# One word per load instead of one per row, and the weights issued behind the barrier: a router kernel

## The chip, the core and the metric

The kernel runs on one core of a Trainium2 chip. The core has five engines with an instruction stream each: TensorE (PE in the profile; PEld is its weight load), VectorE (DVE), ScalarE (ACT), GpSimd (POOL) and SyncE (SP). They meet at semaphores only. DMAs are issued by SyncE, ScalarE or GpSimd and run on sixteen DMA engines. The metric is the device time in microseconds (us), the median of several runs.

## The reference

```python
batch, seq, dim = 16, 512, 1024;  num_loras = 8          # x, router_weights: float32
logits = np.matmul(x, router_weights)                     # 8192 x 1024 times 1024 x 8
exp_logits = np.exp(logits - np.max(logits, axis=-1, keepdims=True))
return (exp_logits / np.sum(exp_logits, axis=-1, keepdims=True)).astype(np.float32)
```

A tall matrix product with eight columns, and a softmax over each row of eight. The input is 32 MB and the output 0.26 MB.

## The kernel before

The 8192 rows are laid out as 128 partitions by 64; "row j" means the j-th row of every partition, so a row is a tile of 128 x 1024 elements. Rows 0 to 3 come as float32 into `x_f32` (two DMAs of SyncE) and ScalarE casts them. All other rows are cast to bfloat16 by the DMA itself, issued by GpSimd: twelve loads of four rows, three of two, five of one (`LOADS`), and row 63 in three pieces of four, two and two eighths (`PIECES`). Each load has its own semaphore, `s_ld[i]` or `s_z[i]`. GpSimd issues all of them in the first 17 us, without waiting for anything but the barrier.

Work on a row: TensorE transposes its eight 128 x 128 chunks (a "turn", against `identity`), into PSUM. VectorE copies five of them to SBUF (`xTv`, L378) and ScalarE three (`xTs`, L351). Then TensorE multiplies the eight transposed chunks with the weights (`multiply`, L238) into eight columns of `lg`. After each group of eight rows VectorE and ScalarE make the softmax between their copies. The last four rows are done one by one (`alone`), the last of them in pieces (L310, L324), and SyncE stores the output in two DMAs (L160, L162).

The order on every engine is written by hand. TensorE's main part is a loop of 31 trips of two rows, with addresses in registers. A trip is: `loop_turn(1)` for an odd row, `multiply` of the even row before it, `loop_turn(0)` for the next even row, a branch, two filler matmuls, and `multiply` of the odd row. The buffers alternate by the parity of the row.

Three things are touched here:

- **Words.** TensorE is told by SyncE that a row of x is there. For each row from 2 to 62 SyncE waits for the load (or the cast) if the row begins one, and adds one to a semaphore (L157): for an even row to `s_in`, for which TensorE waits ahead of `loop_turn(0)` (L295); for an odd row to `s_c[1]`, which also counts the two copies of the odd row before it. So the multiply of an odd row waits for three: its own two copies, and the word of the next odd row (`want=3`). So that this count isn't run ahead of, SyncE waits for `s_tv`, TensorE's count of turned rows, ahead of each odd row.
- **The first turn.** It waits for two casts (`s_cast`, L275).
- **The weights.** ScalarE issues their load (L137) beside SyncE's two loads of x_f32, before `tc.close()` (L144), which makes all engines meet at a barrier. TensorE turns the weights as soon as they and `ident` are there (L268 to L270), and VectorE casts them to `w_bf`.

Of the kernel before, what the change touches and what calls it, by code (L numbers as in the profile page):

```python
# [11 lines left out]
def kernel(  # L12
# [6 lines left out]
    nc = tc.nc  # L19
# [5 lines left out]
    KO = D // P  # L25
    J = M // P
# [13 lines left out]
    LOADS = [4] * 13 + [2, 2, 2] + [1] * 5  # L40
# [14 lines left out]
    def sb(name, shape, dtype):  # L55
        size = mybir.dt.size(dtype)
        for n in shape[1:]:
            size *= n
        at = place[0]
        place[0] = -(-(at + size) // 64) * 64  # L60
        return nc.alloc_sbuf_tensor_at(name, shape, dtype, offset=at).ap()
# [9 lines left out]
    w8 = sb("w8", [KO, P, N], fp32)  # L71
# [24 lines left out]
    sem = tc.alloc_semaphore  # L96


    s_f = [nc.alloc_semaphore(f"s_f{i}") for i in range(2)]
    s_w = nc.alloc_semaphore("s_w")  # L100
    s_ld = [sem(f"s_ld{i}") for i in range(len(LOADS))]
    s_z = [sem(f"s_z{i}") for i in range(len(PIECES))]
    s_cast = sem("s_cast")
# [7 lines left out]
    s_tv = sem("s_tv")  # L111
    s_ts = sem("s_ts")
    s_c = [sem(f"s_c{i}") for i in range(2)]
    s_in = sem("s_in")
# [10 lines left out]
    first = [sum(LOADS[:i]) for i in range(len(LOADS))]  # L125
# [3 lines left out]
    with tc.manual_schedule():  # L129
        early = [  # L130
            nc.sync.dma_start(
                out=x_f32[:, 2 * i:2 * i + 2, :], in_=x_rows[:, 2 * i:2 * i + 2, :]
            ).then_inc(s_f[i], 16)
            for i in range(2)
        ]
        early.append(
            nc.scalar.dma_start(  # L137
                out=w8, in_=router_weights.rearrange("(ko ki) n -> ko ki n", ko=KO)
            ).then_inc(s_w, 16)
        )  # L140
        for t in early:
            tc.no_tile_sem_insts.add(t.ins.name)
    tc.close()
# [2 lines left out]

    sp = nc.sync


    for j in range(2, J - 1):  # L150
        if j % 2:
            sp.wait_ge(s_tv, j - 1)
        if j < LOADS[0]:
            sp.wait_ge(s_cast, j + 1)
        elif j in first:
            sp.wait_ge(s_ld[first.index(j)], 16)
        sp.sem_inc(s_c[1] if j % 2 else s_in, 1)  # L157
    sp.wait_ge(s_z[0], 16)
    sp.wait_ge(s_out, NG - 1)
    sp.dma_start(out=out_rows[:, 0:DONE, :], in_=outv[:, 0:DONE, :]).then_inc(s_st[0], 16)  # L160
# [6 lines left out]
    for i, r in enumerate(LOADS):  # L167
        if i:
            nc.gpsimd.dma_start(  # L169
                out=xa[:, first[i]:first[i] + r, :], in_=x_rows[:, first[i]:first[i] + r, :]  # L170
            ).then_inc(s_ld[i], 16)
        if i == 2:
# [3 lines left out]
                out=ident, in_=ident, compare_op=ALU.not_equal, fill=1.0, base=0,  # L176
# [10 lines left out]
    pe = nc.tensor  # L187
# [7 lines left out]
    def at(ap, like, r):  # L195
        return mybir.RegisterAccessPattern(
            ap=ap, dtype=like.dtype, memsetref=like.tensor.name + "_set",
            regref=r.name, is_regloc_offset=False, reg_ap_offset=r.name,
            const_ap_offset=0, const_sub_tensor_id=0,
        )  # L200

    def again(like, **k):
        return pe.add_instruction(copy.replace(like, name=f"I-{nc.next_id()}", **k))

    def turn_ap(b, c):
        return (ptv if c < VN else pts)[b][:, c if c < VN else c - VN, :]

    def chunk(b, c):
        return xTv[b][:, c, :] if c < VN else xTs[b][:, c - VN, :]

    def loop_turn(b):

        for c in range(KO):
            t = again(
                turn_like,
                ins=(turn_like.ins[0], at([[J * D, P], [1, P]], xa, r_x[c])),
                outs=(pe.lower_ap(turn_ap(b, c), opt=False),),
            )
            if c == VN - 1:
                t.then_inc(s_tv, 1)  # L220
            if c == KO - 1:
                t.then_inc(s_ts, 1)
        pe.reg_add(r_l, r_l, 256)
        for c in range(KO):
            if c == KO // 2:
                pe.reg_alu(r_l, r_l, -4097, ALU.bitwise_and)
            pe.reg_add(r_x[c], r_x[c], D * 2)
# [7 lines left out]
                t.then_inc(s_ts, 1)  # L235
        return t

    def multiply(b, dst, want=2):  # L238

        for c in range(KO):  # L240
            if c == 0:
                pe.wait_ge(s_c[b], want).then_inc(s_c[b], -want)
            if dst is None:
                m = again(
                    mult_like,
                    ins=(
                        pe.lower_ap(w_bf[:, c, :], opt=False),
                        pe.lower_ap(chunk(b, c), opt=False, for_matmul_weights=True),
                    ),
                    outs=(at([[2 * G * 64, P], [1, N]], lg, r_l),),  # L250
                    start_tensor_calc=(c == 0),
                    stop_tensor_calc=(c == KO - 1),
                )
            else:
                m = pe.matmul(  # L255
                    dst, lhsT=chunk(b, c), rhs=w_bf[:, c, :],
                    start=(c == 0), stop=(c == KO - 1),
                )
            if c == KO - 1:
                m.then_inc(s_p, 1)  # L260

    def fill():
        return pe.matmul(spare, lhsT=filler[:, 0:P], rhs=filler, start=True, stop=True)  # L263
# [1 line left out]

    w_ps = lg[:, 1, 0:N, 0:KO]
    pe.wait_ge(s_id, 1)
    pe.wait_ge(s_w, 16).then_inc(s_w, -16)  # L268
    for n in range(N):
        t = pe.transpose(w_ps[:, n, :], w8[:, :, n], ident[0:KO, 0:KO])  # L270
    t.then_inc(s_wt, 1)
    pe.wait_ge(s_fill, 1)
    mult_like = fill().ins
    pe.wait_ge(s_idb, 1)
    pe.wait_ge(s_cast, 2)  # L275
    turn_like = pe.transpose(turn_ap(0, 0), xa[:, 0, 0:P], identity).ins  # L276
    turn(0)
    pe.wait_ge(s_wb, 1)
# [2 lines left out]
    def left_of(i):  # L281

        return X_AT + D * 2 * (2 * i + 3) + (P - 1) * 2
# [3 lines left out]
    with nc.body("rows_multiply", valid_engines=only_pe):  # L287
        fill()
        fill()
        multiply(1, None, want=3)  # L290
        pe.br("rows_turn")
    with nc.body("rows_turn", valid_engines=only_pe):
        loop_turn(1)
        multiply(0, None)
        pe.wait_ge(s_in, 1).then_inc(s_in, -1)  # L295
        loop_turn(0)
        pe.br_lt(r_x[0], left_of(TRIPS - 1), on_true="rows_multiply", on_false="rows_done")
    nc.switch_bb("rows_done")
# [14 lines left out]
    pe.wait_ge(s_c[(J - 3) % 2], 2)  # L313
    turn_piece(0)
    multiply((J - 3) % 2, alone[1])
    turn_piece(1)
    turn_piece(2)
# [13 lines left out]
    act = nc.scalar  # L331

    def cast(i):
        act.wait_ge(s_f[i], 16).then_inc(s_f[i], -16)  # L334
        for k in (2 * i, 2 * i + 1):
            act.copy(xa[:, k, :], x_f32[:, k, :]).then_inc(s_cast, 1)  # L336
# [12 lines left out]
    def act_copy(j):  # L349
        act.wait_ge(s_ts, j + 1)  # L350
        act.copy(xTs[j % 2], pts[j % 2][:, 0:SN, :]).then_inc(s_c[j % 2], 1)  # L351

    cast(0)
    for j in range(J - 3):
        act_copy(j)
# [67 lines left out]
    for j in range(J - 3):  # L423
# [26 lines left out]
        out=outv[:, J - ALONE:J, :], in0=ev3, in1=inv3.broadcast_to([P, ALONE, N]), op=ALU.mult  # L450
# [31 lines left out]
```

## Time and profile before

| | |
|---|---|
| runs before | 86.65, 86.79, 86.89, 86.90 us; median 86.84 |
| profiled execution | 86.75 us, of which its span is 85.4 |
| busy | PE 64.1 us (75%), PEld 52.7 (62%), DVE 38.9 (46%), ACT 38.1 (45%), POOL 13.5 (16%) |
| HBM read, written | 33.59 MB, 0.26 MB |
| x_f loads | two of 1024 KB, issued from 0.74, 4.8 and 8.0 us to landing |
| three pieces of row 63 | issued from 15.0 to 16.1, 65.6 to 65.9 us to landing |
| mean granted TensorE clock | 0.977 of full speed |

The profile is one execution; its times are microseconds from its first instruction. Busy time is by engine. A group or wait names the line, the engine, the operation and the tiles (output before the arrow, input after it). In a waits view, "A <- B: total, times, longest" says that A waited for B. In a timeline the columns are the start, the duration, the engine (a q behind it means its instruction queue), the line, the operation, the tiles and, in brackets, the idle time before it with what ended that. The strip of 40 slices gives the busy share in tenths (9 is 90% or more). The queue lines give packets, MB, and the time of the packets as a share of sixteen engines' span. The trace also holds each DMA packet's start and duration by queue, and the times at which DMAs add to their semaphores; a load has landed when the last of them has come.

### The profile page before, as it was taken

To read this page: it belongs to the slowest core of one execution; us is meant where nothing else is said; L and a number is where in the kernel's file an instruction comes from. 1 tells how busy PE (TensorE), PEld (TensorE's weight loads), DVE (VectorE), ACT (ScalarE), POOL (GpSimd) and SP (SyncE) were. 2 spreads that over 40 slices of the span, in tenths; PEclk is the share of its full clock that TensorE was granted. 3 is DMA by queue.
4 is the path that set the end of the run, shared out by engine and by line. 5 is a ranking of instruction groups with operands and counts; after the bars stand their busy time and mean duration, and the time that the engine had idled before them with its cause. 6 is when DMAs were issued, how large, how long until landed. Compare 5 with 4: busy or idle time off the path is not lost. (4 is left out here: it accounts for less than half of the span.)

```text
span 85.4 us, 2849 instructions
## 1 busy us (share of the span) xinstructions
PE 64.1 (75%) x1094; PEld 52.7 (62%) x1094; DVE 38.9 (46%) x114; ACT 38.1 (45%) x81; POOL 13.5 (16%) x30
## 2 busy tenths in 40 slices
PE   0052739999995977949389997959598699999860
PEld 0040727888874755838258785847476488777650
DVE  0020222466574542745226554636347257665662
ACT  0039385454663352535223454524426246545470
POOL 0489999800000000000000000000000000000000
PEclk9999999999999999999975999999999999999998
DMA  2999999999999999999999999999999999999920
GB/s 58 338 430 307 230 188 238 192 238 199 234 196 234 196 234 196 238 196 234 199 230 203 226 207 222 215 215 219 211 219 198 213 215 215 198 211 208 172 101 23
DMA packets 3906, 18.14 MB, mean 212 GB/s; under 512 B 568, under 2 KB 1080, under 8 KB 2112
## 3 DMA queue, kind: packets, MB, share of 16 engines
q0 software_dynamic: 3312, 15.73, 90.1%
q1 hardware_dynamic: 576, 2.36, 7.2%
q10 hardware_dynamic: 16, 0.03, 0.2%
q14 instruction: 2, 0.02, 0.0%
HBM read 33.59 MB, written 0.26 MB: 396 GB/s over the span
## 5 line engine op out<-in xcount | busy, mean ns | idle before, releaser
L351 ACT COPY xTs<-pts 128x384 bf16<-128x384 bf16 x63 | 30.1, 479 | 38.1 <-PE pts L276 36.8
L378 DVE COPY xTv<-ptv 128x640 bf16<-128x640 bf16 x63 | 31.0, 492 | 34.0 <-PE ptv L276 29.8
L276 PE MATMUL ptv<-identity,x_all 128*128 128x128 bf16 x311 | 29.1, 226 | 12.5 <-SPq L157 8.5
L276 PEld LDWEIGHTS ptv<-identity,x_all 128*128 (+1 forms) x311 | 19.1, 100 | 13.7 <-issue 13.5
L276 PE MATMUL pts<-identity,x_all 128*128 128x128 bf16 x186 | 21.7, 228 | 0.0
L263 PEld LDWEIGHTS lg<-w_bf,xTv 128*128 128x128 bf16 x305 | 15.7, 99 | 8.1 <-issue 2.1
L263 PE MATMUL spare<-filler 128*128 128x512 bf16 x61 | 19.8, 407 | 0.6
L263 PE MATMUL lg<-w_bf,xTv 128*128 128x8 bf16 x305 | 16.7, 167 | 0.0
L276 PEld LDWEIGHTS pts<-identity,x_all 128*128 x186 | 13.9, 103 | 0.0
L263 PE MATMUL lg<-w_bf,xTs 128*128 128x8 bf16 x183 | 13.2, 166 | 0.0
L169 POOL DMA_DIRECT2D x_all<-in_x_dram x20 | 10.8, 602 | 2.8 <-POOLq L144 2.8
L263 PEld LDWEIGHTS lg<-w_bf,xTs 128*128 128x128 bf16 x183 | 9.0, 96 | 0.0
L263 PEld LDWEIGHTS spare<-filler 128*128 128x128 bf16 x61 | 4.6, 103 | 2.4 <-issue 2.3
L270 PE MATMUL lg<-ident,w 8*128 8x8 f32 x8 | 1.0, 251 | 5.3 <-PEq L268 5.3
L270 PEld LDWEIGHTS lg<-ident,w 8*128 8x128 f32 x8 | 0.9, 197 | 5.3 <-issue 5.3
L336 ACT CAST x_all<-x_f 128x1024 bf16<-128x1024 f32 x4 | 4.0, 1044 | 0.0
L336 ACT ACT_TABLE_LOAD x1 | 1.3, 1283 | 5.6 <-ACTq L334 5.6
L386 DVE TENSOR_REDUCE mx<-lg 128x8 f32<-128x64 f32 (+1 forms) x8 | 1.8, 221 | 4.3 <-PE lg L263 4.3
L372 DVE CAST identity<-ident 128x128 bf16<-128x128 f32 x1 | 0.5, 518 | 5.3 <-POOL ident L175 5.3
L341 ACT ACTIVATE ev<-ex 128x64 f32<-128x64 f32 (+1 forms) x8 | 2.0, 253 | 1.1 <-DVE ex L390 1.0
L182 POOL DMA_DIRECT2D x_all<-in_x_dram x3 | 1.7, 687 | 0.0
L390 DVE TENSOR_TENSOR ex<-lg,mx 128x64 f32<-128x64 f32 (+1 forms) x8 | 1.7, 212 | 0.0
(41 smaller groups left out, 15.9 us busy)
## 6 DMA issues: line engine op xcount, KB each, us to landing
x_all<-in_x_dram POOLq DMA_DIRECT2D x12, 1024.0 KB, 32.6
x_f<-in_x_dram SPq DMA_DIRECT2D x2, 1024.0 KB, 6.4
x_all<-in_x_dram POOLq DMA_DIRECT2D x3, 512.0 KB, 60.2
x_all<-in_x_dram POOLq DMA_DIRECT2D x5, 256.0 KB, 64.3
out_dram<-outv SPq DMA_DIRECT2D x1, 208.0 KB, 1.9
x_all<-in_x_dram POOLq DMA_DIRECT2D x1, 128.0 KB, 65.9
x_all<-in_x_dram POOLq DMA_DIRECT2D x2, 64.0 KB, 65.7
out_dram<-outv SPq DMA_DIRECT2D x1, 48.0 KB, 1.6
```

What stands on the lines that cost most here:

```text
L169: nc.gpsimd.dma_start(out=xa[:, first[i]:first[i] + r, :], in_=x_rows[:, first[i]:first[i] + r, :]).then_inc(s_ld[i], 16)
L182: nc.gpsimd.dma_start(out=xa[:, J - 1, c], in_=x_rows[:, J - 1, c]).then_inc(s_z[i], 16)
L263: return pe.matmul(spare, lhsT=filler[:, 0:P], rhs=filler, start=True, stop=True)
L270: t = pe.transpose(w_ps[:, n, :], w8[:, :, n], ident[0:KO, 0:KO])
L276: turn_like = pe.transpose(turn_ap(0, 0), xa[:, 0, 0:P], identity).ins
L336: act.copy(xa[:, k, :], x_f32[:, k, :]).then_inc(s_cast, 1)
L341: act.activation(ev[g % 2][:, 0:n, :], ex[g % 2][:, 0:n, :], func=Exp).then_inc(s_ev, 1)
L351: act.copy(xTs[j % 2], pts[j % 2][:, 0:SN, :]).then_inc(s_c[j % 2], 1)
L372: dve.tensor_copy(out=identity, in_=ident).then_inc(s_idb, 1)
L378: dve.tensor_copy(out=xTv[j % 2], in_=ptv[j % 2][:, 0:VN, :]).then_inc(s_c[j % 2], 1)
L386: dve.reduce_max(mx[b][:, 0:n, 0], rows, axis=X).then_inc(s_d, 1)
L390: dve.tensor_tensor(out=ex[b][:, 0:n, :], in0=rows, in1=mx[b][:, 0:n, :].broadcast_to([P, n, N]), op=ALU.subtract,).then_inc(s_ex, 1)
```

## The change

SyncE now adds to `s_in` alone: one for each of the four casts, and for every other load as many as it has rows, in one instruction when the load lands. It no longer looks at `s_tv`. TensorE takes one from `s_in` ahead of every turn, odd or even, so the wait goes into `loop_turn` itself; the multiply of an odd row waits for its two copies only. The first turn takes one from `s_in` too. The load of the weights goes from before the barrier to the head of ScalarE's own program behind it, ahead of the casts; its semaphore is one that the context clears, so TensorE no longer subtracts from it. The order of matmuls, copies and loads on each engine is the same in both kernels.

```diff
-    s_w = nc.alloc_semaphore("s_w")
+    s_w = sem("s_w")
...
-        early.append(
-            nc.scalar.dma_start(
-                out=w8, in_=router_weights.rearrange("(ko ki) n -> ko ki n", ko=KO)
-            ).then_inc(s_w, 16)
-        )
...
-    for j in range(2, J - 1):
-        if j % 2:
-            sp.wait_ge(s_tv, j - 1)
-        if j < LOADS[0]:
-            sp.wait_ge(s_cast, j + 1)
-        elif j in first:
-            sp.wait_ge(s_ld[first.index(j)], 16)
-        sp.sem_inc(s_c[1] if j % 2 else s_in, 1)
+    for j in range(LOADS[0]):
+        sp.wait_ge(s_cast, j + 1)
+        sp.sem_inc(s_in, 1)
+    for i, r in enumerate(LOADS):
+        if i:
+            sp.wait_ge(s_ld[i], 16)
+            sp.sem_inc(s_in, r)
...
     def loop_turn(b):
 
+        pe.wait_ge(s_in, 1).then_inc(s_in, -1)
         for c in range(KO):
...
-    def multiply(b, dst, want=2):
+    def multiply(b, dst):
...
-                pe.wait_ge(s_c[b], want).then_inc(s_c[b], -want)
+                pe.wait_ge(s_c[b], 2).then_inc(s_c[b], -2)
...
-    pe.wait_ge(s_w, 16).then_inc(s_w, -16)
+    pe.wait_ge(s_w, 16)
...
-    pe.wait_ge(s_cast, 2)
+    pe.wait_ge(s_in, 1).then_inc(s_in, -1)
...
-        multiply(1, None, want=3)
+        multiply(1, None)
...
         multiply(0, None)
-        pe.wait_ge(s_in, 1).then_inc(s_in, -1)
         loop_turn(0)
...
+    act.dma_start(
+        out=w8, in_=router_weights.rearrange("(ko ki) n -> ko ki n", ko=KO)
+    ).then_inc(s_w, 16)
     cast(0)
```

## The prediction

> **What bounds the kernel now.** I read the page first, for the share of the DMA queues and the strip of the 40 slices.
>
> ```profile
> span 85.4 us, 2849 instructions
> ...
> DMA  2999999999999999999999999999999999999920
> GB/s 58 338 430 307 230 188 238 192 238 199 234 196 234 196 234 196 238 196 234 199 230 203 226 207 222 215 215 219 211 219 198 213 215 215 198 211 208 172 101 23
> ...
> q0 software_dynamic: 3312, 15.73, 90.1%
> q1 hardware_dynamic: 576, 2.36, 7.2%
> q10 hardware_dynamic: 16, 0.03, 0.2%
> ```
>
> The sixteen DMA engines are full from the second slice to the 38th. Queue 1 carries rows 0 to 3 (x_f32) and the stores, queue 0 the other rows, queue 10 the weights: 0.2% of the engines' time. TensorE is busy 75%, VectorE and ScalarE 46% and 45%. So the load stream looks like the bound; the chain that ended last covers only 80.48 us onward and cannot say so. The waits do, TensorE's first, then SyncE's queue (total us, times, longest):
>
> ```profile
> PE ptv L276 <- SPq L157: 8.5, 8, 1.8
> ...
> SPq L157 <- DMA x_all<-in_x_dram: 36.6, 19, 3.7
> SPq L157 <- PE ptv L276: 27.7, 17, 2.4
> ```
>
> TensorE waits for SyncE's word, and SyncE for a load. Its second wait, 27.7 us for s_tv, only paces words of rows that are there already. The timeline shows that TensorE has caught up by 27.66:
>
> ```profile
> 0.74 0.58 ACTq L137 DMA_DIRECT2D w<-in_router_weights_dram  x1
> 0.74 0.86 SPq L131 DMA_DIRECT2D x_f<-in_x_dram  x2
> ...
> 5.32 1.01 PE L270 MATMUL lg<-ident,w 8*128 8x8 f32 x8 [5.32 <-PEq L268]
> ...
> 9.03 0.27 PE L276 MATMUL ptv<-identity,x_all 128*128 128x128 bf16 x1 [2.16 <-ACT x_all L336]
> ...
> 27.66 0.44 PE L276 MATMUL ptv<-identity,x_all 128*128 128x128 bf16 x5 [0.99 <-SPq L157]
> ...
> 80.52 0.44 PE L276 MATMUL ptv<-identity,x_all 128*128 128x128 bf16 x5 [0.30 <-PEq L295]
> ...
> 81.71 0.28 PE L310 MATMUL extra<-identity,x_all 128*128 128x128 bf16 x2
> ...
> 83.82 0.34 SPq L162 DMA_DIRECT2D out_dram<-outv  x1
> ```
>
> The same idle time follows with nearly every four-row load (1.06 before 32.52, 1.07 before 37.44, 1.81 before 43.06). At the end row 62 lands at 80.35 by the trace's semaphore records and is turned at 80.52. The last quarter row (s_z[2]) lands at 81.67 and is turned at 81.71. From that landing to the end of the span are 85.4 - 81.67 = 3.7 us that the diff does not touch. So end = end of the load stream + 3.7 us.
>
> **The change, part by part.** The sum is made on the profiled execution: 86.75 us, of which 85.4 are span and 1.35 lie around it. It is 0.09 below the median of the four runs, 86.84; the forecast is put on the median.
>
> *The words of SyncE.* 61 row words become 24 (four for the casts, twenty for loads). One costs 17 ns when it does not wait, on a queue that is not the bound. Row 62 still has a load and a word of its own (lands 80.35, SyncE's instruction at 80.37), so the last one is no sooner. Worth nothing.
>
> *The wait of an odd turn.* It leaves multiply's `want=3` and becomes an instruction in loop_turn(1): 31 more waits, at 51 ns each by the row of the same kind (L295), 1.6 us of TensorE's sequencer. Behind each queue that turn, the next multiply and the next even turn; VectorE and ScalarE wait for these. Per four-row load that is two, 0.10 us, under an idle time of 1.06 us. Every such load begins with an even row, whose wait stays where it is. Only rows 59 and 61 begin a load with an odd row. There the multiply of row 59 runs sooner: two fills from 78.67 at the usual 0.216 us spacing would let it start near 79.10 instead of 79.23, so up to 0.13 us. Row 62, which lands at 80.35 whatever TensorE does, takes that back. TensorE had 0.30 us of idle time before it. Worth nothing on the path; without this cover at most two waits, +0.10.
>
> *The first rows.* Turn 0 needs one cast instead of two. The two casts run from 6.90 to 8.89, so it may start about 1 us sooner than 9.03. It is hidden: what TensorE gains there it waits away at 27.66.
>
> *The weights, start-up side.* ScalarE leaves the barrier at 2.73 and issues then, 2.0 us later than now. Its first cast waits for rows 0 and 1 until 5.53, so the 0.58 us of issue hide there. In this trace the weights land 2.20 us after their issue starts (0.74 to 2.94); with the same delay they land at 4.95, ahead of ident, which lets the transposes start at 5.3. As an upper bound I take the longest x_f load, 8.0 us from issue to landing: 10.75. Then transposes (1.0) and fill (0.6) end at 12.4, and turn 0 is 3.4 us late. The idle times at 27.66, 32.52, 37.44 and 43.06 add up to 4.93 us, so that also is gone long before the end. I take the lower value, because x_f packets are short (0.31 us each).
>
> [...]
>
> *The weights, stream side.* This is the only part that reaches the bound. Eight packets of 4 KB, on eight of the sixteen engines, leave the start and enter the full stretch. The price on an engine: half an 8 KB x_f packet, 0.5 x 309 = 155 ns, if bytes rule; the mean of the eight packets themselves, 0.35 us, if their own row does; nothing, if none of the eight engines is the one that ends last. They now run from 1.70 on, and the first x_f packet starts at 1.89, so part of that time was free. I take +0.155, the price of a packet in the full stretch, where these now lie.
>
> *x_f without the weights beside it.* SyncE's first issue takes 381 ns beside ScalarE's, its second 417; its two stores, alone, 344 and 343. The first x_f packet comes 1.14 us after its issue, the weights' 0.96, a store's 0.84 (81.00 to 81.84). So the stream may start 0 to 0.30 us sooner. A store reads SBUF and a load HBM, so the weights' 0.96 is the nearer row: 0.19 at most, and I take half, -0.09. It can't be a loss, since nothing is put ahead of x_f. The barrier waits for SyncE (its drain at 1.65), so POOL's first load may move with it by the 0.11 that the two issues could save; its first packet at 7.11 finds the engines full anyway.
>
> [...]
>
> Sum: 0 + 0 + 0 + 0.155 - 0.09 = +0.06 us. 86.84 + 0.06 = 86.9.
>
> **The rivals.** (1) *The weights hold up the engine that ends last.* Place: the stretch from 3.7 to 7.6 us, where x_f fills every engine. Price: 0.35 us a packet, 0.71 the longest of the eight. It decides if one of the eight engines is the last to land s_z[2]; those landings spread from 81.07 to 81.67, so a late engine elsewhere would hide it. For it: the load stream has no idle slice to absorb anything. Against: these engines carry the same packets now. Time 86.84 + 0.35 = 87.2, without any gain of x_f; 87.5 with the longest packet.
>
> (2) *x_f starts sooner and the weights land on engines with time to spare.* -0.19 to -0.30: 86.65 to 86.55. For it: x_f's lag behind the weights' packets. Against: its first packets take 0.44 to 0.77 us instead of 0.31, which looks like the start of HBM reads and would stay.
>
> (3) *The change does not reach the bound at all:* the words only rename waits for the same landings, and the weights' bytes are merely shifted within a full stream. 86.84, within the noise of the four runs (86.65 to 86.9). My forecast is this case with a small cost.
>
> (4) *The clock.* It was halved from 43.92 to 47.33, just after the 1.81 us idle time. Were it halved over the last rows, 16 transposes from 80.52 on would take 107 instead of 55 ns each: +0.8, 87.7. Nothing in the change makes idle time at the end longer, so this is a small chance.
>
> **How the numbers follow.** About 0.2%, 0.17 us, is what a measurement of this kernel can tell from no change. Within it, the forecast and rival 3: 0.45. Rival 1 with its sizes 0.28 and rival 4 0.05, together slower 0.33. Rival 2: 0.22. The range runs from 86.5, below the whole 0.30 of rival 2, to 87.4, which takes in the mean price of rival 1 and leaves out its longest packet and the clock. The likeliest case alone would be 86.67 to 87.01.
>
> **What would show it.** Right: the last load lands within 0.2 us of 81.67; TensorE's waits for SyncE's word on even rows stay near 1.06 us; SyncE's wait for s_tv (27.7 us) is gone and the time is not; weights land before 5.3 and turn 0 starts near 8. Rival 1: the landings of all queue 0 loads lie 0.3 later from the first on. Rival 2: the first x_f packet comes before 1.75 and the loads all land sooner. Wrong altogether: TensorE stops waiting for loads, or the time from the last landing to the end is no longer 3.7 us.

## The result, and the profile after

The changed kernel takes 86.98 us (median of 40 runs, 86.87 to 87.40), the kernel before 86.88 in its 64 runs of the same session. The ratio is 1.0018, 95% interval 1.0013 to 1.0024: 0.16 us slower, as the means are (87.04 and 86.88), while the medians are 0.10 apart. Six of the 40 runs make up the difference. They lie by themselves at 87.30 to 87.40, with spans of 86.0 to 86.1, and none of the 64 of before is over 87.04; the mean of the other 34 is 0.10 above that of before. What sets the six apart is not known, and the kept profile is not one of them. The profiled execution of the changed kernel took 87.0 us, 85.7 of them span; before it was 86.75 and 85.4.

First the page of the changed kernel: the head, the strip of the sixteen DMA engines in 40 slices, and the queues.

```profile
span 85.7 us, 2843 instructions
...
DMA  4799999999999999999999999999999999999920
GB/s 61 317 421 317 229 199 229 199 229 210 222 214 214 218 210 226 203 229 203 233 195 233 203 226 203 229 199 233 195 233 189 214 214 214 204 210 208 154 101 23
...
q0 software_dynamic: 3312, 15.73, 89.8%
q1 hardware_dynamic: 576, 2.36, 7.5%
q10 hardware_dynamic: 16, 0.03, 0.1%
```

The engines are full from the third slice to the 38th; the second shows seven tenths where it had nine. Queue 10 shows the weights: the same bytes, but 0.1% of the engines' time where it was 0.2%, so the packets have become shorter. The waits (in all, times, longest) of TensorE and of SyncE's queue:

```profile
PE ptv L270 <- PEq L206: 11.1, 11, 1.8
PE lg L264 <- DMA w<-in_router_weights_dram: 7.9, 1, 7.9
...
SPq L150 <- DMA x_all<-in_x_dram: 66.2, 19, 5.6
SPq L146 <- ACT x_all L329: 10.9, 4, 5.3
```

TensorE's idle time now carries the name of its own wait in `loop_turn` (L206), behind which stands SyncE's word. SyncE's 27.7 us of waiting for TensorE (`s_tv`) are gone. They have gone into its waits for loads, which rose from 36.6 to 66.2 us: SyncE waits as much as before, for the loads alone. New is TensorE's wait for the weights, 7.9 us. The timeline shows the start, the caught-up stretch and the end:

```profile
0.74 0.86 SPq L131 DMA_DIRECT2D x_f<-in_x_dram  x2
2.79 0.58 ACTq L346 DMA_DIRECT2D w<-in_router_weights_dram  x1
...
7.94 1.01 PE L264 MATMUL lg<-ident,w 8*128 8x8 f32 x8 [7.94 <-DMA w<-in_router_weights_dram]
...
9.29 0.31 PE L270 MATMUL ptv<-identity,x_all 128*128 128x128 bf16 x1
...
27.88 0.44 PE L270 MATMUL ptv<-identity,x_all 128*128 128x128 bf16 x5 [0.61 <-PEq L206]
...
32.76 0.44 PE L270 MATMUL ptv<-identity,x_all 128*128 128x128 bf16 x5 [1.07 <-PEq L206]
...
80.78 0.44 PE L270 MATMUL ptv<-identity,x_all 128*128 128x128 bf16 x5 [0.42 <-PEq L206]
...
81.97 0.29 PE L303 MATMUL extra<-identity,x_all 128*128 128x128 bf16 x2
...
84.08 0.34 SPq L155 DMA_DIRECT2D out_dram<-outv  x1
```

Three things are to be seen. The first turn comes at 9.29, later than the 9.03 of before. From 27.88 on TensorE waits for loads as it did. And everything at the end is 0.26 us later: turn of row 62 at 80.78 against 80.52, last pieces at 81.97 against 81.71, last store at 84.08 against 83.82. So the 0.26 us of span (85.69 against 85.43) were lost before the last landing.

The trace's packet and semaphore records say where. Times are us from the span's start.

| | before | after |
|---|---|---|
| weights issued | 0.74 | 2.79 |
| weights' packets start | 1.70 to 1.79 | 6.23 to 6.76 |
| one weights packet of 4 KB | 0.156 to 0.707, mean 0.351 | 0.159, all eight |
| weights landed | 2.94 | 7.81 |
| first x_f packet starts | 1.885 | 1.748 |
| first GpSimd load lands, from and to | 12.51, 12.88 | 12.58, 13.12 |
| last quarter row lands (`s_z[2]`), from and to | 81.07, 81.67 | 81.11, 81.93 |
| last landing to the end of the span | 3.76 | 3.76 |

The first landing of the first GpSimd load is 0.08 later and its last 0.24 later; at the last quarter row these are 0.04 and 0.26. So the delay against the kernel before is there at 13 us and lasts to the end.

The packet records carry no engine number, but packets that follow one another without a gap can be strung into sixteen chains. In the changed kernel the eight chains with a weights packet end their eighth queue-0 packet at 12.54 on the mean (latest 12.80), the eight others at 12.37 (latest 12.52). Before, the two groups stood near 12.39, within 0.05 of each other; some joints of the chains are open, and the means of before are no better than that. So the late engines are those that carry the weights. But one profile is one draw, as the run late_start below shows; the sizes need the runs.

The engine that ends last seems to have a second burden, which neither my prediction nor my theory priced. Two 8 KB packets of instructions (queue 14, 322 ns each) run at 41.5 and 49.5 us before, and at 41.7 and 48.7 after. Up to the load that lands at 37 us, the last of the sixteen landings of a load comes 0.37 to 0.38 us behind the first before, and 0.51 to 0.54 after. From the load at 51 us on these are 0.59 to 0.68 and 0.80 to 0.86. In the traces of all twelve kernels the spread grows at the time of these packets, by 0.1 to 0.4 us, and stays so. The engine that lands last is therefore most likely one that also carries an instruction packet. If which engines carry these packets changes from run to run, so does the part of the weights' delay that shows at the end; the records don't say.

### The profile page after: what moved, and what is told of

Read it like the earlier page. It is cut to its first block, busy times and chain, and to the rows that moved or that the text cites. A ratio compares the mean times of both kernels' runs of the same rounds, so it can differ in the third digit from the quotient of the medians.

```text
span 85.7 us, 2843 instructions
## 1 busy us (share of the span) xinstructions
PE 63.0 (74%) x1094; PEld 52.0 (61%) x1094; DVE 38.9 (45%) x114; ACT 38.0 (44%) x81; POOL 13.4 (16%) x30
## 5 line engine op out<-in xcount | busy, mean ns | idle before, releaser
L270 PE MATMUL ptv<-identity,x_all 128*128 128x128 bf16 x311 | 28.6, 224 | 11.2 <-PEq L206 11.1
## 6 DMA issues: line engine op xcount, KB each, us to landing
x_all<-in_x_dram POOLq DMA_DIRECT2D x1, 128.0 KB, 66.2
```

## The experiments

The theory, A: the weights' packets now lie in the full stretch of the load stream, on eight of sixteen engines, and push what ends last on these back by about a packet. The rivals: B, the new words and waits cost; C, the late weights cost through TensorE's late start (first turn 9.29), not through the stream. Ratios are to the kernel before on the same chip, with the 95% interval.

**The halves of the change.** words_only has the words and waits of the changed kernel, and the weights issued ahead of the barrier as before:

```diff
+        early.append(nc.scalar.dma_start(out=w8, in_=...).then_inc(s_w, 16))
...
-    act.dma_start(out=w8, in_=...).then_inc(s_w, 16)
```

> The words of after, the weights issued early as before. Stream theory (the late weights put 0.159 us on eight DMA engines in a full stretch, and one of these then lands last): ratio to before 1.0000 within 0.0005, about 86.88 us; last landing of s_z[2] as before, 81.67 within 0.1. Words theory (31 more waits of TensorE and the coarser words cost the time): 1.0015, about 87.0. Start-up theory (the late weights make TensorE's first turn late, and this carries to the end): 1.0000.

Measured: 86.93 us (11 runs), ratio 1.0004 [0.9995, 1.0013]. Its timeline at the start and at the end:

```profile
0.74 0.57 ACTq L137 DMA_DIRECT2D w<-in_router_weights_dram  x1
...
8.17 0.27 PE L275 MATMUL ptv<-identity,x_all 128*128 128x128 bf16 x1 [1.28 <-PEq L274]
...
80.64 0.44 PE L275 MATMUL ptv<-identity,x_all 128*128 128x128 bf16 x5 [0.45 <-PEq L211]
...
81.84 0.28 PE L308 MATMUL extra<-identity,x_all 128*128 128x128 bf16 x2
```

The first turn is 0.86 us sooner than before (8.17 against 9.03) and the end is no sooner; `s_z[2]` lands at 81.79, a little outside the 0.1 that I had allowed. Words and odd-turn waits cost nothing that can be measured, and their earlier start earns nothing: B falls.

weights_only is the other half: the words of before, the weights behind the barrier.

```diff
-        early.append(nc.scalar.dma_start(out=w8, in_=...).then_inc(s_w, 16))
...
+    act.dma_start(out=w8, in_=...).then_inc(s_w, 16)
```

> The words of before, the weights issued by ScalarE behind the barrier. Stream theory: as after, ratio 1.0012 to 1.0030, 87.0 to 87.15, landings of every GpSimd load about 0.2 us later from the first one on. Words theory: 1.0000. Start-up theory: 1.0015 with landings as before.

Measured: 87.68 us (6 runs), ratio 1.0096 [1.0081, 1.0112]. That is five times what the whole change costs, and no theory expected it. Inside its profile there is nothing of that size: the span is 85.6 and `s_z[2]` lands at 81.84. But the execution took 87.46, so 1.84 us lie outside the span of 85.62 (1.86 with the span rounded, as in the expectations below), where before and after have 1.31 to 1.32. The trace has one 8 KB packet of instructions (queue 14) after the last instruction, at 87.21; before and after have none there. The half thus can't be read from its time alone; its spans are read below.

**Padding the end of that program.** weights_only_pad adds 8 increments of an unused semaphore to SyncE's program, weights_only_pad32 adds 32:

```diff
+    for _ in range(8):        # 32 in weights_only_pad32
+        sp.sem_inc(s_pad, 1)
     sp.wait_ge(s_z[0], 16)
```

> weights_only with eight more instructions on SyncE's queue that nobody waits for. weights_only spent 1.86 us outside its span instead of 1.35, with an 8 KB packet of the instruction queue after its last instruction. If that is a matter of where the program ends in its instruction memory, the time outside the span changes with the padding and comes to 1.3 to 1.4 at best, ratio 1.0012 to 1.0030; the stream inside the span stays as in weights_only, last landing 81.8 to 81.95. If it belongs to the late weights with the row words: 1.009 again.

Measured: 87.38 us (5 runs), ratio 1.0052 [1.0039, 1.0066]; span 85.7, 1.61 outside. The extra instruction packet is now at 82.33, inside the span.

> weights_only with 32 more semaphore increments in SyncE's program at its end (weights_only_pad had 8), ahead of the wait for the last load. If the time that weights_only shows outside its span (1.86 us, 1.62 with eight) comes of where the end of the program lies among its fetched instructions, it moves again: the time less the span is back near 1.3, the span stays 85.5 to 85.8, and the ratio is 1.0012 to 1.0030, which is the late weights alone. If the words of before and the late weights cost more together than apart for another reason, the time less the span stays at 1.6 to 1.9 and the ratio at 1.005 to 1.010.

Measured: 87.36 us (5 runs), ratio 1.0058 [1.0045, 1.0071]; span 85.7, 1.60 outside. The extra packet is at 82.62. Eight increments took 0.2 us off the time outside the span, 24 more nothing, and the return to 1.3 us that I expected did not come. Every run also has its span on record. The means are 85.85 us (weights_only, 6 runs), 85.74 and 85.76 (5 runs each), against 85.57 to 85.58 for the runs of before beside them and 85.73 for the changed kernel. So inside the span the late weights alone cost 0.16 to 0.28 us, about what A expected (0.10 to 0.26) and as much as the whole change (0.16); the extra time is not the weights' place in the stream. What the time outside the span is stays open; the changed kernel does not show it, with a time less span of 1.27 to 1.36 us in each of its recorded runs (spans to a tenth).

**No weights at all.** no_weights leaves the load of the weights out and lets VectorE fill `w8` with a constant, so its logits are others:

```diff
-    act.dma_start(out=w8, in_=...).then_inc(s_w, 16)
+    dve.memset(w8, 0.5).then_inc(s_w, 16)
```

> After without the load of the weights: VectorE fills the tile with a constant instead, so the logits are not the reference's. Stream theory: the 0.159 us leave the eight engines, and x_f starts as soon as in after; ratio 0.9990 to 1.0002, 86.80 to 86.90, last landing 81.5 to 81.7. Words theory: 1.0015 as after. Start-up theory: 1.0000 or a little less, since TensorE has its weights early, with landings as in after.

Measured: 87.2 us (12 runs), ratio 1.0048 [1.0022, 1.0073], in two groups: six runs from 86.92 to 87.02, six from 87.39 to 87.89. Its profile is of the upper group, 87.7 us with a span of 85.3: again it is time outside the span, 2.4 us, here with a 16 KB packet of instructions on another queue (8) at 86.67, after the last instruction. Inside, `s_z[2]` lands at 81.61, 0.32 before the changed kernel's, as A expects of the absent packets. As a time it decides nothing. Its spans do: 85.3 to 85.5 in all twelve runs, mean 85.43, which is 0.30 below the changed kernel and 0.14 below the runs of before beside it. The second figure suggests that the early weights had a cost of their own.

**More of the suspected cost.** weights_x4 loads the weights three more times, into tiles that are not used, on the same eight partitions; the store at the end waits for them as well.

```diff
+    for wx in more:
+        act.dma_start(out=wx, in_=router_weights.rearrange("(ko ki) n -> ko ki n", ko=KO)).then_inc(s_more, 16)
```

> After with three more loads of the weights into tiles that nothing reads, right behind the first one on ScalarE's queue. Stream theory: 3 x 0.159 = 0.48 us more on the same eight engines than in after: ratio to before 1.006 to 1.0075, 87.4 to 87.55, the last landing 0.4 to 0.5 us later than in after. Start-up and words theories: as after, 1.0018, since the weights that are used still come first and TensorE's waits are the same.

Measured: 87.89 us (4 runs), ratio 1.0119 [1.0104, 1.0134], time less span 1.31. The head of its page, its queue 10, and the last pieces in its timeline:

```profile
span 86.5 us, 2847 instructions
...
q10 hardware_dynamic: 64, 0.13, 0.5%
```

```profile
82.83 0.28 PE L306 MATMUL extra<-identity,x_all 128*128 128x128 bf16 x2
```

The last piece is turned at 82.83, 0.86 later than in the changed kernel, or 0.29 per copy; the medians are 0.91 apart. That is nearly twice the 0.48 that A had priced. The sixteen landings of the first GpSimd load fall into two groups of eight, 12.57 to 12.81 and 13.25 to 13.93. Their means, 12.71 and 13.48, are 0.77 apart, 0.19 per copy of four, which is what a later packet and its 4-byte write take in this trace (172 and 22 ns). This is A's mark: eight engines are late, by a packet and a write for each copy, which makes 0.58 for the three. The end follows the latest of them: the last landing of all, 82.79, is 0.86 after the changed kernel's. The other 0.3 goes with that one engine, which is 0.46 behind the mean of its group (13.93); why, is not shown.

**The same bytes over sixteen engines.** x4_wide is weights_x4 with the three extra loads laid over 16 partitions, which is meant to put 2 KB of a copy on each engine. spread16 is the changed kernel with its one load laid out in that way; TensorE then turns the weights in two halves, with 16 small matmuls (32 records in the trace) in place of the eight transposes.

```diff
-    w8 = sb("w8", [KO, P, N], fp32)
+    w8 = sb("w8", [2 * KO, P // 2, N], fp32)
...
-        t = pe.transpose(w_ps[:, n, :], w8[:, :, n], ident[0:KO, 0:KO])
+        for h in range(2):
+            t = pe.matmul(w_ps[h * H:(h + 1) * H, n, :], lhsT=w8[:, :, n], rhs=ident[0:2 * KO, h:2 * KO:2], ...)
...
-        out=w8, in_=router_weights.rearrange("(ko ki) n -> ko ki n", ko=KO)
+        out=w8, in_=router_weights.rearrange("(q r) n -> q r n", q=2 * KO)
```

> After with three more loads of the weights into tiles that nothing reads, each over sixteen partitions of 2 KB. The bytes are those of weights_x4. Stream theory: three packets of 0.08 us and three completion writes of 0.02 on each engine, 0.3 us, so ratio to before 1.0045 to 1.0065, about half of what weights_x4 (1.0119) lost over after, with one group of sixteen landings instead of two groups of eight. If it is the queue's work and not the load on the last engine: as weights_x4, 1.012.

Measured: 87.28 us (5 runs), ratio 1.0042 [1.0028, 1.0056]. Its page and its last pieces:

```profile
span 86.0 us, 2847 instructions
...
q10 hardware_dynamic: 112, 0.13, 0.5%
```

```profile
82.32 0.29 PE L306 MATMUL extra<-identity,x_all 128*128 128x128 bf16 x2
```

With the same bytes on queue 10, the three copies now cost 0.35 us beyond the changed kernel (82.32 - 81.97), not 0.86: less than half, and by the medians 0.30 in place of 0.91. The ratio is just under the range that I gave. The sixteen landings of the first GpSimd load show no gap between two groups, but they spread over 0.80 us (12.87 to 13.67).

> After with the weights in 16 partitions of 64 rows instead of 8 of 128, so that their load makes one 2 KB packet on each of the sixteen engines and not one of 4 KB on eight; TensorE turns them with 16 small matmuls instead of 8 transposes, 1 us more at the start. Stream theory: 0.08 us on every engine instead of 0.159 on eight, so about half of what the late weights cost: ratio to before 1.0000 to 1.0014, and the landings of the first GpSimd load spread by at most 0.45 us instead of 0.54. Start-up theory: no better than after, 1.0018 or more, since the first turn comes another 1 us later.

Measured: 86.90 us (11 runs), ratio 1.0000 [0.9991, 1.0009]; its interval lies wholly below that of the changed kernel. Its timeline:

```profile
2.80 0.38 ACTq L351 DMA_DIRECT2D w<-in_router_weights_dram  x1
...
7.91 2.09 PE L266 MATMUL lg<-ident,w 16*64 16x8 f32 x32 [7.91 <-DMA w<-in_router_weights_dram]
...
10.34 0.31 PE L275 MATMUL ptv<-identity,x_all 128*128 128x128 bf16 x1
...
81.85 0.29 PE L308 MATMUL extra<-identity,x_all 128*128 128x128 bf16 x2
```

The weights are issued as late as in the changed kernel, and the first turn is a further 1.05 us later (10.34), and yet the 0.18% are gone. The packets take 84 ns each, sixteen in the place of eight, and the first load lands within 0.33 us (12.75 to 13.08) in place of 0.54. This speaks for A and against C at once.

**The late start by itself.** late_start is words_only with six filler matmuls ahead of the first turn:

```diff
+    for _ in range(6):
+        fill()
     turn_like = pe.transpose(turn_ap(0, 0), xa[:, 0, 0:P], identity).ins
```

> words_only (weights early) with six more filler matmuls of TensorE ahead of its first turn: at the cold rate 0.43 us each, 2.6 us in all, so the first turn comes at 9 to 11 us or later than in after. Stream theory: 1.0004 as words_only, since TensorE's idle time at each four-row load takes it back by 45 us. Start-up theory: slower by what the first turn is late, 0.1 us or more for each 0.26 us in after's proportion (0.16 us of time for 0.26 us of delay).

Measured: 86.95 us (11 runs), ratio 1.0004 [0.9995, 1.0013], as words_only to the last digit.

```profile
9.24 0.31 PE L277 MATMUL ptv<-identity,x_all 128*128 128x128 bf16 x1
...
12.89 0.44 PE L277 MATMUL ptv<-identity,x_all 128*128 128x128 bf16 x5 [1.45 <-PEq L211]
...
81.92 0.29 PE L310 MATMUL extra<-identity,x_all 128*128 128x128 bf16 x2
```

With the first turn at 9.24 TensorE starts within 0.05 us of the changed kernel, and the time does not move; it waits 1.45 us ahead of 12.89 all the same: C falls. The last line is a warning. In this one execution the end lies at 81.92, as late as in the changed kernel, with the weights issued early. Their packets took 0.77 to 1.14 us here, against a mean of 0.51 in words_only and 0.35 before, and the eight chains that carry them end their eighth queue-0 packet near 12.6, the others near 12.4. So early weights can cost their engines as much as late ones. In the profiles of before and words_only their engines were less than 0.1 behind; with the late weights they were behind by 0.15 to 0.20, in the changed kernel, in weights_only and in its two padded forms. The medians hold the difference, and a single profile does not.

**A version that might beat both.** early16 is words_only with the weights early and over 16 partitions.

> words_only (TensorE's one word per turn, weights issued before the barrier), with the weights laid over 16 partitions, so that 16 DMA engines carry 2 KB each instead of eight carrying 4 KB. Theory of the full stream: the weights' 159 ns on eight engines become about 84 ns on sixteen, all ahead of x_f; ratio 0.9990 to 1.0004, which is the same as before; the first GpSimd load's landings spread over at most 0.4 us. Rival, that the weights' place after the barrier is what costs, however they are spread: also the same as before, since they are early here. A gain over 0.2% would say that the early weights cost before something that no step of mine priced.

Measured: 86.93 us (12 runs, 86.68 to 87.39), ratio 1.0005 [0.9991, 1.0020]. Fifteen of its packets take 84 ns and one 229, from 2.43 on, and `s_z[2]` lands at 81.84. These packets too lie behind the first of x_f (1.75), although they were issued at 0.74, so the version did not put them ahead of the stream as I had expected. It gains nothing that can be measured: the first GpSimd load lands within 0.24 us, and from 51 us on, after the instruction packets, the spread is 0.60 to 0.62, as before.

## Why the prediction was right, step by step

The forecast, 86.9 us with its likeliest case at "within 0.2%", held: 86.98, ratio 1.0018. The step that carried it was the right one. Of the others, one was mis-sized and one had an error that is hidden. As a change the forecast was small: +0.06 us, where the medians say +0.10 and the ratio +0.16.

- **The words of SyncE and the wait of an odd turn, nothing:** shown by words_only, 1.0004. Row 62 did take back what rows 59 and 61 might win: it lands at 80.62 and is turned at 80.78.
- **The first rows, hidden:** shown by words_only (first turn 0.86 sooner, no gain) and late_start (1.07 later than that, no loss).
- **The weights, start-up side:** the landing was wrong and its cost right. I took 4.95 from the issue-to-landing time of before; they landed at 7.81, between that and my upper bound of 10.75. The initial step is as before: the first addition to `s_w` comes 0.68 us after the issue starts (3.47 against 2.79; before 1.40 against 0.74). But the packets start 3.44 us after the issue, not 0.96. In the packet chains an engine has carried 12 to 14 of its 16 x_f packets by then, where I had expected the weights soon, x_f packets being short (0.31 us). Behind the weights packet there is then room for one x_f packet: on at least six of the eight engines the 4-byte write that ends the load starts 0.46 to 0.47 us after the start of the weights packet, which leaves room for that packet's 0.159 and one x_f packet of 0.309. So what I had wrong is how long the weights' first packet takes to start. The trace of before had the sign: GpSimd issued the first load of queue 0 at 3.29, its first packet came at 7.11, and only nine of the 256 x_f packets started after it. No run varies the number of packets ahead, so the cause of the late start stays open. The late landing is hidden as the step said: spread16 starts an additional 1.05 us later and loses nothing.
- **The weights, stream side, +0.155:** right in mechanism and near in size. A weights packet in the full stretch takes 159 ns, and its engines fall 0.17 behind the others (chains of the changed kernel) or 0.19 per copy (weights_x4). The ratio's 0.18% is 0.16 us. That it meets 0.155 so closely is in part luck: the ratio also holds the gain of x_f, whatever is left of it, and the six long runs; and the end follows the latest engine, by 0.26 us in the two profiles, and not the mean of the eight. The place and the choice of engine are those of rival 1, whose price, the 0.35 us mean of the early packets, was the wrong row: that is what a packet costs at the start.
- **x_f sooner, -0.09:** mis-sized. The first x_f packet does start 0.137 sooner, within the 0.19 that I had as the upper end, but its first sixteen packets then take 0.60 to 1.33 us, against 0.31 to 0.77 before. The engines without weights end their eighth queue-0 packet at 12.37, against some 12.4: about 0.03 are left, if any. This was the argument against rival 2 ("the start of HBM reads"), and it should have had more weight. SyncE's first issue takes 383 ns alone and took 381 beside ScalarE's, so no wait of the one for the other is to be seen there. With 0.03 in the place of 0.09 the sum is +0.125, between the +0.10 of the medians and the +0.16 of the ratio. (The sum started from 86.84, the median of four runs; the 64 runs have 86.88.)
- **The last 3.7 us:** untouched, 3.76 in the changed kernel. The granted clock is full over the last rows, so rival 4 did not come:

```profile
79.37:84.42 5.05, 2.98 (x65) 2.57 (x63) 3.26 (x16) 2.56 (x8) 0.00 (x0) 1.00 0.52 103
```

This is the windows view of the changed kernel: the window and its length, the busy time and number of instructions of PE, PEld, DVE, ACT and POOL, the granted clock (1.00), the DMA share and GB/s.

Of the signs that I named, TensorE's waits near 1.06 us (1.07 before 32.76) and the vanished `s_tv` wait came. The weights did not land before 5.3, nor did turn 0 start near 8. The last landing is 0.26 from 81.67 where I allowed 0.2. And the landings are 0.24 later from the first GpSimd load on, which I had named as the sign of rival 1. Of rival 2's signs one came by a hair, the first x_f packet at 1.748 where I had "before 1.75"; the loads did not land sooner.

That early weights cost less than late ones is seen in the spans too (no_weights is 0.14 below before and 0.30 below the changed kernel). Why is only argued: part of their time lies before x_f's first packet (from 1.70 against 1.885 in before), which the late ones can't use.

## What to carry to other kernels

In a kernel that its load stream bounds, what an edit does to words, waits and the first turns was worth nothing here (words_only and late_start, 1.0004), where the compute engine waits for loads later on. What it puts into the full stretch of the stream cost about its packet's duration there, on the engines that carry it, and the end follows the latest engine, which can be further behind (0.29 us per copy in weights_x4, for packets of 0.17). A small load on few partitions made those engines late to the end of the kernel (0.17 us behind the others in the changed kernel's chains, its last landing 0.26 later than before): issue it ahead of the stream (words_only, 1.0004), or lay it over sixteen partitions (spread16, 1.0000). With both, in early16, it gained nothing more (1.0005). A load issued a little later than a long one can start far later than its issue (3.44 us here, 0.96 before), so its landing is not the old delay moved along. And a difference in time is read beside the span: weights_only lost 0.5 us outside it, of which the load stream shows nothing.

## What the runs showed of the hardware that I had not expected

- Packets of a DMA on ScalarE's queue started 3.44 us after its issue, when SyncE's loads had 12 to 14 of 16 packets per engine done; without these ahead it was 0.96. On at least six of the eight engines the load's 4-byte write started 0.46 to 0.47 us after the start of the weights packet, which leaves room for that packet's 0.159 and one x_f packet of 0.309.
- Two kernels that differ little from the others have more time outside the span: 1.84 us in weights_only (1.61 with eight more instructions of SyncE, 1.60 with 32) and 2.4 in no_weights, against 1.31 to 1.32 in the other profiles. The three forms of weights_only have a third 8 KB instruction packet near or after the end, and no_weights has one of 16 KB at 86.67, after its last instruction. But early16 has one of 16 KB too, at 83.34, and 1.32 us outside its span. What that time is stays open.
- The same 4 KB packet, issued early, took from 0.156 to 1.14 us in the profiles of three kernels that issue it alike; in the full stretch the eight of the changed kernel took 159 ns each.
- Two 8 KB instruction packets in the middle of the kernel (322 ns each) come when the spread of a load's sixteen landings grows, from 0.38 to 0.6 us before and from 0.54 to 0.8 in the changed kernel, and it stays so to the end. That they are the cause is read from the times alone.
